# Hybrid decoder on one core: another order of score tiles, key tiles, bias rows and memory work in the mixer, and jobs of projection on both sides of each head's transposes

## The chip, the cores and the metric

The kernel runs on one core of a Trainium2 chip. The time is the device time of one launch in microseconds; lower is better. Engines are named as in the profile: PE is TensorE (matmuls; PEld its weight loads), DVE is VectorE, ACT is ScalarE, POOL is GpSimd, SP issues the loads from memory (DMA).

## What is computed

Two layers on x of 512 tokens by 1024 channels in float32. The change lies in the second of a layer's four parts, the mixer, and in what the mixer prepares for the third.

```python
# per layer
x = x + 0.5 * swiglu(rmsnorm(x, g_ffn1[l]), w_ffn1_gu[l], w_ffn1_down[l])
h = rmsnorm(x, g_mix[l])
zb, zc, zv, zq, zk, zval, zf = jnp.split(h @ w_mix_in[l], SPLITS, axis=-1)
y_conv = zb * causal_depthwise_conv(zc * zv, w_conv[l])          # 512 channels, 3 taps
log_f = jax.nn.log_sigmoid((zf + b_f[l]).astype(jnp.float32))    # 8 heads of 64
# forgetting attention: softmax(q k^T / sqrt(64) + c_t - c_s, causal) v, c = cumsum(log_f)
y_att = forgetting_attention(q, k, v, log_f)
y = jnp.concatenate([rmsnorm(y_conv, g_conv_out[l]), rmsnorm(y_att, g_att_out[l])], axis=-1)
x = x + y @ w_mix_out[l]
x = x + memory_cross_attention(rmsnorm(x, g_xattn[l]), rmsnorm(mem, g_mem[l]), w_xq[l], w_xkv[l], w_xo[l])
x = x + 0.5 * swiglu(rmsnorm(x, g_ffn2[l]), w_ffn2_gu[l], w_ffn2_down[l])
# after the last layer: rmsnorm(x, g_final)
```

## The kernel before

Activations lie transposed, channels on the 128 partitions and 512 tokens along a row. Every product of an activation with a weight is made of float32r matmuls of split operands: `mm3` (L204) does high by high, high by low and low by high, three matmuls of 128x512. `split` (L208 on ACT, L209 on DVE) makes the two halves of an activation; `Weights.prefetch` (L157 on ACT, L158 on DVE) those of a weight unit of 128x1024, two jobs ahead of its use, into three unit buffers. SP loads the raw weights in the order of a list that the kernel writes down ahead of each part (`W.block`).

The kernel is written through a recorder which decides, from the order of the code and from costs of its own, how the instructions of an engine follow one another; each engine then goes through its own list in order. A matmul of a projection can thereby stand between two score matmuls that come earlier in the code.

The mixer first projects v and the forget gate (96 matmuls and `pf`, L778). What is left are jobs of 24 matmuls, in the list `MIX`: q and k of a pair of heads (`head_rows`), or one of the three projections of a conv group (`Conv.step`, L671 to L685). The order is q0 k0 zc0 zv0 zb0 zc1 q1 k1 zv1 zb1 q2 k2 zc2 zv2 q3 k3 zb2 zc3 zv3 zb3. The first five run ahead of head 0 (`MIX_FIRST`); then a loop over h = 0 to 9 does `scores(h)`, some jobs (`MIX_STEP[h]`), `weigh(h - 2)` and `turn(h - 1)`.

- `head_rows`: DVE scales the product (L804). For k, ACT casts the high half of each head's 64 rows (L821), DVE subtracts the low half (L822), ACT copies the high half to the other 64 partitions (L825) and writes the bias rows c times a coefficient next to the low half (L826). So the contraction of a score is over 128 rows, and its two matmuls (e = 0 and 1, L838) need L821 and L825, then L822 and L826.
- `forget_bias` (L701 to L726): from the gate to c by an exp and a log (two ACT table loads, L708 and L709), a scan (L713) and the bias rows of q (L722). It is called in the job k0.
- `scores(h)`: four row tiles t of 128 queries against 128 (t + 1) keys, mask and row maximum on DVE (L840), exp on ACT (L844), reciprocal on DVE (L847), normalising on POOL (L849). By `by_size` the tiles of 128 and 384 keys share one PSUM tile and one SBUF tile.
- `turn(h)`: ten transposes on PE (L859), split on ACT and DVE (L865, L866). `weigh(h)`: eight matmuls of the key tiles kt with v (L875), and L882, L883.
- The memory of the third part: `memory_load` after head 4, `memory_norm` (squares on ACT, L945; L949, L952) after head 6, `memory` (16 transposes, L964; L215, L216) at h = 8, keys (`memory_keys`, matmuls of 128x256, L985, L986) behind the loop, in turn with the sums and the spreading of the two output norms (L391, L395, L407, L411), values behind the output projection.

Of the kernel before, what the change touches and what calls it, by code (L numbers as in the profile page):

```python
# [12 lines left out]
P = 128  # L13
# [5 lines left out]
KD = D // P  # L19
CW = 512  # L20
NT = S // P
NH = 8
# [149 lines left out]
def trunk(ctx, tc, a, consts, out):  # L172
# [14 lines left out]
    def PS():  # L187
        return pspool.tile([P, 512], F32, name="ps", tag="ps")
# [75 lines left out]
    W = Weights(nc, big_pool, unit_pool)  # L264
    for l in range(DEPTH):
        for which in (1, 2):
            gu, dn = a[f"w_ffn{which}_gu"][l], a[f"w_ffn{which}_down"][l]
            if which == 2:
                w_in, w_out = a["w_mix_in"][l], a["w_mix_out"][l]
                W.limit = 4  # L270
                for k in range(4):
                    W.block(w_in, 2 * k, 2, (2560, 512))
                for kind, i in MIX:
                    W.block(w_in, 0, KD, (MIX_COL[kind] + P * i, P))
                for c in range(KD):
                    W.block(a["w_xkv"][l], 0, KD, (P * c, P))
                for c in range(KD):
                    W.block(w_out, 0, KD, (P * c, P))
                for c in range(2):
                    for k in range(4):  # L280
                        W.block(a["w_xkv"][l], 2 * k, 2, (D + 512 * c, 512))
                W.limit = BIG_BUFS - 4
                for n in ("w_xq", "w_xo"):
                    for c in range(KD):
                        W.block(a[n][l], 0, KD, (P * c, P))
                W.slow = 10
            W.limit = BIG_BUFS - 2
            product = {}
            for op, c, i in ffn_plan():
                c0 = sum(CHUNKS[:c])  # L290
                if op == "plain":
                    W.block(gu, 2 * i, 2, (c0, 256), (DFF + c0, 256))
                elif op == "product":
                    if c not in product:
                        product[c] = W.quads(gu, c0, CHUNKS[c])
                    product[c](i)
                elif op == "down" and l == DEPTH - 1 and which == 2 and c == len(CHUNKS) - 1:
                    W.limit = 4
                    W.unit(W.raw(dn, c0 // P + 2 * (i % 2), 2, (512 * (i // 2), 512)), keep=True)
                elif op == "down":  # L300
                    W.block(dn, c0 // P, CHUNKS[c] // P, (256 * i, 256))
# [387 lines left out]
    def scaled(y, norm, base):  # L689

        for i, t in enumerate(y):
            nc.vector.scalar_tensor_tensor(
                out=t, in0=t, scalar=col(base + i), in1=norm.rb, op0=ALU.mult, op1=ALU.mult
            )
            yield split(t)
# [60 lines left out]
    def mixer(l, n, after):  # L756
# [4 lines left out]
        pv = [PS() for _ in range(NT)]  # L761
        wf = None
        for c in range(4):
            w = W.take()
# [18 lines left out]
        v = []  # L783
# [16 lines left out]
        def head_rows(kind, p):  # L800
            ps = PS()
            project(ps, W.take(), n.h)
            t = T()
            nc.vector.scalar_tensor_tensor(  # L804
                out=t, in0=ps, scalar=64 ** -0.5 if kind == "q" else 1.0, in1=n.norm.rb,
                op0=ALU.mult, op1=ALU.mult,
            )
            if kind == "k" and p == 0:
                c.append(forget_bias(l, n, pf, q))
            for b in (0, 64):  # L810
                r, o = slice(b, b + 64), slice(64 - b, 128 - b)
                if kind == "q":
                    nc.scalar.copy(
                        out=q[b][r, :, :], in_=t[r, :].unsqueeze(1).broadcast_to([64, 2, 512])
                    )
                    nc.vector.tensor_tensor(
                        out=q[b][o, 0, :], in0=t[r, :], in1=q[b][r, 0, :].bitcast(F32), op=ALU.subtract
                    )
                else:
                    hi = k[b][r, 0, :]  # L820
                    nc.scalar.copy(out=hi, in_=t[r, :])  # L821
                    nc.vector.tensor_tensor(  # L822
                        out=k[b][r, 1, :], in0=t[r, :], in1=hi.bitcast(F32), op=ALU.subtract
                    )
                    nc.scalar.copy(out=k[b][o, 0, :], in_=t[r, :])  # L825
                    nc.scalar.activation(  # L826
                        out=k[b][o, 1, :], in_=c[0][o, :], func=AF.Copy, scale=coef(6 + p)[o]
                    )

        def scores(h):  # L830
            b = 64 * (h % 2)
            den, inv = SM(NT), SM(NT)
            w, pss = by_size(T(), T(), T()), by_size(PS(), PS(), PS())
            for t in range(NT):
                m = (t + 1) * P
                ts_, o, ps = slice(t * P, m), w[t], pss[t]
                for e in range(2):
                    mm(ps, q[b][:, e, ts_], k[b][:, e, :m], start=not e, stop=e == 1)  # L838
                neg = SM(1)
                nc.vector.tensor_tensor_reduce(  # L840
                    out=o, in0=ps, in1=cst[:, C_MASK + 512 - m : C_MASK + 512],
                    scale=-1.0, scalar=3.0e38, op0=ALU.add, op1=ALU.min, accum_out=neg,
                )
                nc.scalar.activation(  # L844
                    out=o, in_=o, func=AF.Exp, bias=neg, scale=-1.0, accum_out=den[:, t : t + 1]
                )
            nc.vector.reciprocal(out=inv, in_=den)  # L847
            for t in range(NT):
                nc.gpsimd.tensor_tensor(  # L849
                    out=w[t], in0=w[t], in1=inv[:, t : t + 1].broadcast_to([P, (t + 1) * P]), op=ALU.mult  # L850
                )
            wsm[h] = w
# [16 lines left out]
        def weigh(h):  # L869
            p, b = h // 2, 64 * (h % 2)  # L870
            w = wt.pop(h)
            ps = PS()
            for kt in range(NT):
                for e in range(2):
                    mm(  # L875
                        ps[:, kt * P :], v[kt][:, h, :], w[kt][e],
                        start=kt == e == 0, stop=kt == NT - 1 and e == 1,
                    )
            if not b:
                y[p] = T()  # L880
            o = y[p][b : b + 64, :]
            nc.scalar.copy(out=o, in_=ps[64:, :])  # L882
            nc.vector.tensor_add(out=o, in0=ps[:64, :], in1=o)  # L883
            if b:
                norm.add(y[p])
# [3 lines left out]
        def job(n):  # L889
            for _ in range(n):  # L890
                kind, i = jobs.pop(0)
                (head_rows if kind in "qk" else conv.step)(kind, i)

        job(MIX_FIRST)
        for h in range(NH + 2):
            if h < NH:
                scores(h)
            job(MIX_STEP[h])
            if h >= 2:
                weigh(h - 2)  # L900
            if 1 <= h <= NH:
                turn(h - 1)
            if h == 1:
                scale.change(n.norm)
            if h == 4:
                memory_load()
            if h == 6:
                memory_norm()
            if h == 8:
                m = memory(l)  # L910
        n.h = None
        conv.norm.column()
        kT = memory_keys(m, 0, 2)
        conv.norm.spread()
        norm.column()
        kT += memory_keys(m, 2, 2)
        norm.spread()
        yc = list(scaled(conv.y, conv.norm, 88 + 4 * l))
        kT += memory_keys(m, 4, 2)
        ya = list(scaled(y, norm, 96 + 4 * l))  # L920
        kT += memory_keys(m, 6, 2)
        y = yc + ya
        for j in range(KD):
            ps = PS()
            project(ps, W.take(), y)
            nc.vector.tensor_add(out=x[j], in0=ps, in1=x[j])
            after.add(j)
        return kT, memory_values(m)

    mem_in = {}  # L930

# [57 lines left out]
                kT.append((hi[:, e, :], lo[:, e, :]))  # L989
        return kT  # L990

    def memory_values(m):
        v = [[None, None], [None, None]]
        for c in range(2):
            pv = [PS(), PS()]
            for kc in range(4):
                w = W.take()
                for t in range(2):
                    for k2 in range(2):
                        kk = 2 * kc + k2  # L1000
                        mm3(
                            pv[t], [e[:, t * P : (t + 1) * P] for e in m[kk]], [e[:, k2, :] for e in w],
                            kk == 0, kk == KD - 1,
                        )
            for t in range(2):
                v[t][c] = split(pv[t])
        return v

    def cross_attention(l, n, kT, v, after):
        q = [None] * KD  # L1010
# [170 lines left out]
    _HEADS[0] + _CONV[:4] + _HEADS[1] + _CONV[4:6] + _HEADS[2] + _CONV[6:8] + _HEADS[3] + _CONV[8:]  # L1181
)
MIX_FIRST = 5
MIX_STEP = [1, 3, 1, 3, 1, 3, 1, 1, 1, 0]


def ffn_plan():
# [59 lines left out]
```

## Time and profile before

| | us |
|---|---|
| median of 3 runs (lowest, highest) | 2158.92 (2158.47, 2159.44) |
| the profiled execution | 2158.55 |
| its span, first to last instruction | 2156.8 |
| PE busy, share of the span | 2137.7, 99% |
| DVE busy | 1633.3, 76% |
| ACT busy | 1034.5, 48% |
| POOL busy | 94.1, 4% |

The busy share of an engine is an average over the whole kernel. A matmul's record begins when it enters and ends when its last column has left, so that records of matmuls that follow each other overlap. In the rows an idle time before an instruction stands in brackets with the instruction that ended it.

### The profile page before, as it was taken

To read this page: it belongs to the slowest core of one execution; us is meant where nothing else is said; L and a number is where in the kernel's file an instruction comes from. 1 tells how busy PE (TensorE), PEld (TensorE's weight loads), DVE (VectorE), ACT (ScalarE), POOL (GpSimd) and SP (SyncE) were. 2 spreads that over 40 slices of the span, in tenths; PEclk is the share of its full clock that TensorE was granted. 3 is DMA by queue.
4 is the path that set the end of the run, shared out by engine and by line. 5 is a ranking of instruction groups with operands and counts; after the bars stand their busy time and mean duration, and the time that the engine had idled before them with its cause. 6 is when DMAs were issued, how large, how long until landed. Compare 5 with 4: busy or idle time off the path is not lost.

```text
span 2156.8 us, 26234 instructions
## 1 busy us (share of the span) xinstructions
PE 2137.7 (99%) x10110; PEld 1786.1 (83%) x10110; DVE 1633.3 (76%) x2254; ACT 1034.5 (48%) x1550; POOL 94.1 (4%) x107
## 2 busy tenths in 40 slices
PE   9999999999999999999999999999999999999998
PEld 7888888788888888888888888887888888888887
DVE  7987777768755688888788887767786547977785
ACT  7443434566444554444454443346664445434343
POOL 0000000022001000000000000001320010000000
PEclk9999999999999999999999999999999999999999
DMA  5333332123552133333413333502343521333321
GB/s 180 122 108 108 117 99 68 49 79 106 148 138 88 59 108 109 96 98 98 132 58 113 98 108 98 143 24 69 88 127 110 135 79 49 117 108 118 109 77 40
DMA packets 218371, 214.56 MB, mean 99 GB/s; under 512 B 9230, under 2 KB 167174, under 8 KB 218246
## 3 DMA queue, kind: packets, MB, share of 16 engines
q1 hardware_dynamic: 218214, 212.88, 33.3%
q8 instruction: 79, 1.29, 0.2%
q14 instruction: 46, 0.38, 0.1%
q10 hardware_dynamic: 32, 0.01, 0.0%
HBM read 210.77 MB, written 2.10 MB: 99 GB/s over the span
## 4 chain that ended last, share of the span: by engine, by line
PE 92%; DVE 4%; ACT 3%; issue 1%; POOL 0%; DVEq 0%; POOLq 0%; ACTq 0%
PE ps L204 88%; PE ps L579 2%; DVE wlo L158 1%; ACT whi L157 1%; DVE t L866 1%; ACT t L844 1%; PE ps L838 0%; DVE t L685 0%; DVE t L386 0%; PE ps L778 0%; PE ps L1071 0%; DVE t L883 0%; PE ps L875 0%; PE ps L199 0%; PE ps L391 0%
## 5 line engine op out<-in xcount | busy, mean ns | idle before, releaser
L157 ACT CAST whi<-big 128x1024 fp32r<-128x1024 f32 x516 | 536.7, 1040 | 887.5 <-PE ps L204 692.6
L204 PE MATMUL ps<-t,whi 128*128 128x512 f32 x2752 | 851.8, 390 | 0.3
L204 PE MATMUL ps<-whi,t 128*128 128x512 f32 x2624 | 828.7, 390 | 0.2 <-ACT t L208 0.2
L158 DVE TENSOR_TENSOR wlo<-big,whi 128x1024 fp32r<-128x1024 f32 x516 | 623.7, 1211 | 183.7 <-ACT whi L157 181.6
L204 PEld LDWEIGHTS ps<-t,whi 128*128 128x128 f32 x2752 | 514.8, 188 | 106.8 <-DVE t L209 1.6
L204 PEld LDWEIGHTS ps<-whi,t 128*128 128x128 f32 x2624 | 492.6, 188 | 102.8 <-ACT t L208 0.9
L204 PE MATMUL ps<-t,wlo 128*128 128x512 f32 x1376 | 535.7, 389 | 0.0
L204 PE MATMUL ps<-wlo,t 128*128 128x512 f32 x1312 | 510.5, 389 | 0.0
L204 PEld LDWEIGHTS ps<-t,wlo 128*128 128x128 f32 x1376 | 258.3, 188 | 53.5
L204 PEld LDWEIGHTS ps<-wlo,t 128*128 128x128 f32 x1312 | 246.4, 188 | 50.3
L76 DVE TENSOR_TENSOR big<-big 128x1024 f32<-128x1024 f32 x160 | 193.6, 1218 | 1.7
L589 DVE SCALAR_TENSOR_TENSOR x<-ps,x 128x512 f32<-128x512 f32 x184 | 125.0, 686 | 90.2 <-PE ps L204 90.2
L209 DVE TENSOR_TENSOR t<-ps,t 128x512 fp32r<-128x512 f32 x128 | 82.5, 682 | 24.4 <-ACT t L208 24.0
L369 POOL TENSOR_TENSOR s<-s,mhalf 128x4 f32<-128x4 f32 (+1 forms) x19 | 16.4, 863 | 1728.4 <-DVE s L366 1690.6
L208 ACT CAST t<-ps 128x512 fp32r<-128x512 f32 x128 | 70.7, 602 | 26.0 <-PE ps L204 18.6
L849 POOL TENSOR_TENSOR t<-t,s 128x128 f32<-128x128 f32 (+1 forms) x64 | 58.5, 945 | 215.3 <-DVE s L847 181.1
L527 ACT COPY t<-ps 128x512 f32<-128x512 f32 x80 | 45.8, 586 | 34.1 <-PE ps L204 31.3
L844 ACT ACTIVATE t<-t,s 128x128 f32<-128x128 f32 (+1 forms) x64 | 35.4, 555 | 26.4 <-DVE s L840 26.2
L204 PE MATMUL ps<-big,whi 128*128 128x256 f32 x256 | 47.6, 287 | 0.0
L386 DVE TENSOR_TENSOR t<-t 128x512 f32<-128x512 f32 x61 | 44.2, 725 | 1.4 <-ACT t L382 1.4
L579 PE MATMUL ps<-cst,t 128*128 128x128 f32 x352 | 42.3, 272 | 0.0
L579 PEld LDWEIGHTS ps<-cst,t 128*128 128x128 f32 x352 | 39.8, 141 | 3.0
(177 smaller groups left out, 1638.6 us busy)
## 6 DMA issues: line engine op xcount, KB each, us to landing
big<-in_w_ffn_gu SPq DMA_DIRECT2D x160, 512.0 KB, 3.7
big<-in_w_ffn_down SPq DMA_DIRECT2D x80, 512.0 KB, 3.4
big<-in_w_mix_in SPq DMA_DIRECT2D x48, 512.0 KB, 3.9
big<-in_w_xkv SPq DMA_DIRECT2D x32, 512.0 KB, 3.9
big<-in_w_ffn_gu SPq DMA_DIRECT2D x32, 256.0 KB, 3.2
big<-in_w_mix_out SPq DMA_DIRECT2D x16, 512.0 KB, 4.9
big<-in_w_xq SPq DMA_DIRECT2D x16, 512.0 KB, 3.7
big<-in_w_xo SPq DMA_DIRECT2D x16, 512.0 KB, 4.3
```

The lines of the kernel that those rows point to most:

```text
L76: self.nc.vector.tensor_tensor(out=out, in0=a, in1=b, op=op)
L157: self.nc.scalar.copy(out=hi, in_=src)
L158: self.nc.vector.tensor_tensor(out=lo, in0=src, in1=hi.bitcast(F32), op=ALU.subtract)
L204: mm(ps, x, y, start=first and i == 0, stop=last and i == 2)
L208: nc.scalar.copy(out=hi, in_=src)
L209: nc.vector.tensor_tensor(out=lo, in0=src, in1=hi.bitcast(F32), op=ALU.subtract)
L386: nc.vector.tensor_add(out=self.acc, in0=self.acc, in1=sq)
L527: nc.scalar.copy(out=s[i, e], in_=ps)
L579: nc.tensor.transpose(ps[:, t * P : (t + 1) * P], g[t][:, f * P : (f + 1) * P], ident)
L589: nc.vector.scalar_tensor_tensor(out=x[j], in0=ps, scalar=0.5, in1=x[j], op0=ALU.mult, op1=ALU.add)
L844: nc.scalar.activation(out=o, in_=o, func=AF.Exp, bias=neg, scale=-1.0, accum_out=den[:, t : t + 1])
L849: nc.gpsimd.tensor_tensor(out=w[t], in0=w[t], in1=inv[:, t : t + 1].broadcast_to([P, (t + 1) * P]), op=ALU.mult)
```

## The change

The tiles of `scores` are taken in the order 0, 1, 3, 2 and the key tiles of `weigh` in the order 0, 2, 1, 3. `forget_bias` is called in the job q0. `MIX_STEP` now has two numbers for each h: the jobs between `scores(h)` and `weigh(h - 2)`, and those behind `turn(h - 1)`. The memory is loaded, normed and transposed one head earlier, its first two key units come at h = 8, half of its values ahead of the output projection, between whose units the last two attention rows are scaled, and the weight list follows that order.

```diff
-                for c in range(KD):
-                    W.block(w_out, 0, KD, (P * c, P))
                 for c in range(2):
+                    if c:
+                        for i in range(KD):
+                            W.block(w_out, 0, KD, (P * i, P))
                     for k in range(4):
                         W.block(a["w_xkv"][l], 2 * k, 2, (D + 512 * c, 512))
...
-            if kind == "k" and p == 0:
+            if kind == "q" and p == 0:
                 c.append(forget_bias(l, n, pf, q))
...
-            for t in range(NT):
+            for t in (0, 1, 3, 2):
                 m = (t + 1) * P
...
-            for kt in range(NT):
+            for kt in (0, 2, 1, 3):
                 for e in range(2):
...
-            job(MIX_STEP[h])
+            job(MIX_STEP[h][0])
             if h >= 2:
                 weigh(h - 2)
             if 1 <= h <= NH:
                 turn(h - 1)
+            job(MIX_STEP[h][1])
             if h == 1:
                 scale.change(n.norm)
-            if h == 4:
+            if h == 3:
                 memory_load()
-            if h == 6:
+            if h == 5:
                 memory_norm()
-            if h == 8:
+            if h == 7:
                 m = memory(l)
+            if h == NH:
+                kT = memory_keys(m, 0, 2)
         n.h = None
         conv.norm.column()
-        kT = memory_keys(m, 0, 2)
+        kT += memory_keys(m, 2, 2)
         conv.norm.spread()
         norm.column()
-        kT += memory_keys(m, 2, 2)
+        kT += memory_keys(m, 4, 2)
         norm.spread()
         yc = list(scaled(conv.y, conv.norm, 88 + 4 * l))
-        kT += memory_keys(m, 4, 2)
-        ya = list(scaled(y, norm, 96 + 4 * l))
         kT += memory_keys(m, 6, 2)
+        rest, ya = scaled(y, norm, 96 + 4 * l), []
+        ya += [next(rest), next(rest)]
+        mv = [memory_values(m, 0, lambda kc: ya.append(next(rest)) if 0 < kc < 3 else None)]
         y = yc + ya
...
-        return kT, memory_values(m)
+        mv.append(memory_values(m, 1))
+        return kT, list(zip(*mv))
...
-MIX_STEP = [1, 3, 1, 3, 1, 3, 1, 1, 1, 0]
+MIX_STEP = [(1, 0)] + [(1, 1)] * 6 + [(0, 1), (1, 0), (0, 0)]
```

The number of instructions is the same on every engine (PE 10110). The line numbers of the changed mixer are higher by one, so that L839 of it is L838 of before, L822 is L821, L826 is L825, L827 is L826. Three places show how they are ordered.

PE between k of the second pair and the scores of head 2, before. First the end of the k job (ps_3584) and the next one, the projection zv of conv group 1 (ps_3625):

```order
L204 MATMUL ps_3584<-t_3050,whi_3482 128x512
L204 MATMUL ps_3584<-t_3049,wlo_3483 128x512
L204 MATMUL ps_3625<-t_2885,whi_3548 128x512
L204 MATMUL ps_3625<-t_2886,whi_3548 128x512
L204 MATMUL ps_3625<-t_2885,wlo_3549 128x512
```

PE at the end of that zv job, before: ten transposes of head 0, and then the scores of head 2:

```order
L204 MATMUL ps<-t,wlo 128x512
L859 MATMUL ps<-cst,t 128x128 x10
L838 MATMUL ps<-big 128x128 x2
L838 MATMUL ps<-big 128x256 x2
L838 MATMUL ps<-big 128x512 x2
L204 MATMUL ps<-t,whi 128x512 x2
```

The same k job on PE now (ps_3609), with the scores of head 2 (ps_3665 to ps_3667, from the k rows big_3240 and the q rows big_3238) and zv of group 1 (ps_3693):

```order
L204 MATMUL ps_3609<-t_3050,whi_3482 128x512
L204 MATMUL ps_3609<-t_3049,wlo_3483 128x512
L839 MATMUL ps_3665<-big_3240,big_3238 128x128
L839 MATMUL ps_3666<-big_3240,big_3238 128x256
L839 MATMUL ps_3667<-big_3240,big_3238 128x512
L204 MATMUL ps_3693<-t_2885,whi_3548 128x512
L839 MATMUL ps_3665<-big_3240,big_3238 128x128
L839 MATMUL ps_3666<-big_3240,big_3238 128x256
L839 MATMUL ps_3667<-big_3240,big_3238 128x512
L204 MATMUL ps_3693<-t_2886,whi_3548 128x512
L204 MATMUL ps_3693<-t_2885,wlo_3549 128x512
```

The scores of head 2 moved past a job and the transposes, to the end of the k job whose rows they read; heads 4 and 6 stand likewise behind k of pairs 2 and 3.

ACT at k of the last pair, before (t_4202 is the scaled product, big_3240 and big_3241 the rows of the two heads):

```order
L157 CAST whi_4172<-big_3879 128x1024
L157 CAST whi_4213<-big_3920 128x1024
L821 CAST big_3240<-t_4202 64x512
L825 CAST big_3240<-t_4202 64x512
L821 CAST big_3241<-t_4202 64x512
L825 CAST big_3241<-t_4202 64x512
L157 CAST whi_4322<-big_4024 128x1024
```

The same place on ACT now (the product is t_4241; L951 is L945 of before, the square of a memory tile):

```order
L157 CAST whi_4309<-big_3999 128x1024
L951 ACTIVATE t_4252,s_4251<-t_3953 128x512
L822 CAST big_3240<-t_4241 64x512
L826 CAST big_3240<-t_4241 64x512
L822 CAST big_3241<-t_4241 64x512
L826 CAST big_3241<-t_4241 64x512
L951 ACTIVATE t_4254,s_4251<-t_3955 128x512
```

Squares of the memory's norm now stand in front of and behind the four casts.

ACT from the cast of c (L715) to the first exp of head 0, before (t_3324 is c):

```order
L157 CAST whi_3413<-big_3247 128x1024
L715 CAST t_3327<-t_3324 128x512
L683 ACTIVATE t_3408<-t_3406,gcol_83 128x512
L157 CAST whi_3482<-big_3284 128x1024
L826 ACTIVATE big_3240<-t_3324,cst_76 64x512
L826 ACTIVATE big_3241<-t_3324,cst_76 64x512
L382 ACTIVATE t_3446<-t_3443 128x512
L844 ACT_TABLE_LOAD
L844 ACTIVATE t_3450,s_3448<-t_3450,s_3458 128x128
```

The same stretch now (c is t_3287; L814 casts the q rows of head 1, L716 is L715, L684 is L683 and L383 is L382 of before):

```order
L716 CAST t_3290<-t_3287 128x512
L814 CAST big_3239<-t_3273 64x1024
L822 CAST big_3240<-t_3332 64x512
L826 CAST big_3240<-t_3332 64x512
L827 ACTIVATE big_3240<-t_3287,cst_76 64x512
L822 CAST big_3241<-t_3332 64x512
L826 CAST big_3241<-t_3332 64x512
L827 ACTIVATE big_3241<-t_3287,cst_76 64x512
L684 ACTIVATE t_3408<-t_3406,gcol_83 128x512
L157 CAST whi_3413<-big_3247 128x1024
L157 CAST whi_3482<-big_3306 128x1024
L383 ACTIVATE t_3446<-t_3443 128x512
```

The bias rows moved from behind the second weight cast to a place ahead of the convolution's L684.

## Rows read from the trace of the kernel before

**Rows 1.** Page, busy time of each engine.

```profile
PE 2137.7 (99%) x10110; PEld 1786.1 (83%) x10110; DVE 1633.3 (76%) x2254; ACT 1034.5 (48%) x1550; POOL 94.1 (4%) x107
```

**Rows 2.** Windows: stretch, length; busy PE, PEld, DVE, ACT, POOL; PEclk, DMA share, GB/s.

```profile
362.00:635.00 273.00, 268.46 (x1365) 227.22 (x1364) 192.47 (x321) 154.98 (x264) 34.77 (x38) 1.00 0.36 103
635.00:1425.00 790.00, 789.80 (x3639) 657.92 (x3638) 619.76 (x784) 355.98 (x492) 10.28 (x11) 1.00 0.32 97
1425.00:1700.00 275.00, 270.35 (x1372) 228.61 (x1372) 191.93 (x319) 154.99 (x264) 34.84 (x38) 1.00 0.36 102
```

**Rows 3.** Waits of PE: line, waited for, us in total, times, longest us.

```profile
PE ps L838 <- DVE s L840: 4.9, 8, 1.4
PE ps L838 <- ACT big L826: 2.6, 2, 1.3
...
PE ps L407 <- DVE s L401: 0.8, 2, 0.4
PE ps L875 <- DVE t L866: 0.5, 2, 0.3
```

**Rows 4.** Chain that ended last, in order of time: start, us, what.

```profile
1.45 5.20 PE ps L199 x14
...
98.46 59.87 PE ps L204 x264
```

**Rows 5.** Timeline of PE at the first scores: start, us, instruction, [idle before].

```profile
415.90 0.62 PE L838 MATMUL ps<-big 128*128 128x128 f32 x3
...
419.21 0.72 PE L838 MATMUL ps<-big 128*128 128x128 f32 x3 [1.31 <-ACT big L826]
...
425.20 0.39 PE L204 MATMUL ps<-t,whi 128*128 128x512 f32 x1
427.00 0.62 PE L838 MATMUL ps<-big 128*128 128x384 f32 x2 [1.41 <-DVE s L840]
```

**Rows 6.** Timeline of DVE and ACT at the first scores.

```profile
418.44 1.47 ACT L826 ACTIVATE big<-t,cst 64x512 fp32r<-64x512 f32 x2 [1.52 <-DVE t L726]
...
420.73 0.67 DVE L676 TENSOR_TENSOR t<-t 128x512 f32<-128x512 f32 x1
421.33 0.28 DVE L840 CUSTOM_DVE_ANT_0 t<-ps,cst 128x128 f32<-128x128 f32 x1
...
422.08 1.28 ACT L844 ACT_TABLE_LOAD   x1
...
423.90 0.72 ACT L826 ACTIVATE big<-t,cst 64x512 fp32r<-64x512 f32 x1
...
426.58 0.18 DVE L847 RECIPROCAL s<-s 128x4 f32<-128x4 f32 x1 [1.41 <-ACT t L844]
```

**Rows 7.** Timeline of PE, DVE and ACT behind k of pair 1.

```profile
438.15 0.62 PE L204 MATMUL ps<-t,whi 128*128 128x512 f32 x2
...
438.35 0.69 DVE L804 SCALAR_TENSOR_TENSOR t<-ps,t 128x512 f32<-128x512 f32 x1 [1.87 <-PE ps L204]
...
440.35 1.40 DVE L822 TENSOR_TENSOR big<-t,big 64x512 fp32r<-64x512 f32 x2
...
439.09 0.61 ACT L821 CAST big<-t 64x512 fp32r<-64x512 f32 x1
439.72 0.62 ACT L825 CAST big<-t 64x512 fp32r<-64x512 f32 x1
```

**Rows 8.** Timeline of ACT at the memory's norm.

```profile
514.72 0.66 ACT L945 ACTIVATE t<-t 128x512 f32<-128x512 f32 x1
```

**Rows 9.** Timeline of PE at the end of the first mixer's heads.

```profile
533.13 1.01 PE L875 MATMUL ps<-t,big 128*128 128x512 f32 x2
...
536.06 0.34 PE L204 MATMUL ps<-big,whi 128*128 128x256 f32 x1
```

**Rows 10.** Timeline of PE at the end of the kernel.

```profile
2144.65 4.92 PE L204 MATMUL ps<-big,t 128*128 128x512 f32 x21
```

**Rows 11.** Window behind it, columns as in rows 2.

```profile
2152.00:2157.00 5.00, 0.00 (x0) 0.00 (x0) 1.41 (x2) 0.00 (x0) 0.14 (x1) 0.51 0.28 105
```

More of the change, by code (lines that the diff above doesn't have):

```diff
@@ L990, in memory_keys, with memory_values @@
         return kT
[L992 to L1004, printed above, removed]
-            for t in range(2):
-                v[t][c] = split(pv[t])
-        return v
+    def memory_values(m, c, between=lambda kc: None):
+        pv = [PS(), PS()]
+        for kc in range(4):
+            w = W.take()
+            between(kc)
+            for t in range(2):
+                for k2 in range(2):
+                    kk = 2 * kc + k2
+                    mm3(
+                        pv[t], [e[:, t * P : (t + 1) * P] for e in m[kk]], [e[:, k2, :] for e in w],
+                        kk == 0, kk == KD - 1,
+                    )
+        return [split(ps) for ps in pv]
     def cross_attention(l, n, kT, v, after):
```

## The prediction

> **What bounds the kernel now.** The first view to read is the engine table: TensorE (PE) is busy 2137.7 us of a span of 2156.8 [rows 1]. The change adds and removes no matmul, so only PE's idle time can move, and the second view, windows over whole stages, says where that is: in the stretch of the first mixer 273.00 − 268.46 = 4.54 us of PE is not busy, in that of the second 4.65, while the 790 us between them miss 0.20 [rows 2]. The third view names the waits: L838, the score matmuls, waits 8 times for the mask on VectorE (DVE, L840) and twice for the bias rows (ScalarE, L826); with two waits each at L407 and L875 that makes 14 waits and 8.8 us, half in each mixer [rows 3]. A wait costs more than its idle time. A projection matmul has a record of 0.39 us but follows the one ahead every 59.87 / 264 = 0.227 us [rows 4]; a PE that waits has drained the other 0.163. So a mixer's seven waits cost 4.4 + 7 × 0.163 = **5.5 us**. That is all there is to gain at waits; what replaces them decides.
>
> **The first scores.** PE asks for head 0 at 415.90; the second half of its products stands at 419.21 because of L826, 1.31 us [rows 5]. The change puts the forget bias behind the q projection, one job of 24 × 0.227 = 5.4 us earlier, so the rows are written by about 413, and this wait is gone. But the order of the rows of DVE ahead of the first mask hardly shrinks: it now takes the two scaled convolution taps, two weight splits and L675/L676 behind the second half of the q and k rows. Before, the mask starts at 421.33 [rows 6]; adding the same durations in the new order I get 420.75, end 420.98. The tile of 384 keys shares its buffer with that of 128 keys, and may not start until the mask has read the latter. PE, with 1.47 us less behind it, is there after 13 projection matmuls, at about 419.85: a new wait of about **1.2** (nothing if DVE gets ahead by the 0.5 us of L726, 1.9 if it gets ahead by nothing).
>
> Head 1 waits for the mask too, behind the reciprocal of head 0, and that behind L676, the square L382, an exp table load of 1.28 and four exps. Only the bias row of 0.72 that stood between the exps falls out, so the reciprocal comes at 426.58 − 0.76 = 425.82, PE's release at 426.24 instead of 427.00. PE, which came to this wait at 425.20 + 0.227 = 425.43, now comes there at 425.43 − 1.47 + 1.2 = 425.1: **1.1** in place of 1.41 [rows 5, 6] (0.4 to 1.4).
>
> **The jobs in front of the scores.** Here the change costs. Before, between the k projection of a pair and the first scores of that pair's heads (2, 4, 6) stood a conv projection and ten transposes, over 5 us, and PE had no wait there for key rows [rows 3]. After, the first three score matmuls stand directly behind the last k matmul, and PE takes nothing past them. What they need, for k of pair 1: the next matmul could start at 438.15; DVE scales the product at 438.35 for 0.69 us, ScalarE (ACT) casts the high half from 439.09 and copies it to the other half from 439.72, to 440.34 [rows 7]. With 0.05 us to PE (the first of the two L826 ends at 419.16, PE starts at 419.21 [rows 5, 6]) the first score matmul starts at 440.39: **2.24 us lost**. The low half, L822, ends with its first half near 441.05, 2.9 us behind 438.15; three score matmuls and one of projection cover the difference. I take 2.25 each for heads 2 and 4 (2.2 to 2.9: none of the three steps overlaps another, so none can be shorter; the upper end is PE waiting for L822 as well).
>
> For head 6 the order on ACT has an L945 of 0.66 in front of the cast, since the memory's norm now stands one head earlier [rows 8]; it was issued behind the last cast before. That makes 2.25 + 0.65 = **2.9** (2.2 if L945 is through in time, 4 if two stand there). The norm's other work on DVE and ACT also stands in front of the mask of head 6: 0.5 at the tile of 384 (0 to 0.9). Head 7: 0.2, the sort of small mask wait that three heads show before; heads 3 and 5 nothing.
>
> On PE's order the Trainium skill, "TensorE: Matmul & The Clock Gate", section "Step-by-step: what each phase is for", says that only weight loads are pulled ahead and matmuls stay in program order; the trace agrees, since at 419.21 PE had stood 1.31 us with projection matmuls behind [rows 5]. If matmuls could pass, the sum would be that of the first rival.
>
> **The tail.** The last `weigh`, the norm sums and the first memory keys come in one stretch: from 533.13 to 536.06 PE does eight L875 (1.21 as in other heads), four L391 (0.44) and four 128x256 (0.12 each), 2.13 in 2.93 us [rows 9]. With the keys at head 8 and the memory transposed at head 7 the 0.8 us lost there, and the waits at L407 and L875, should go; I leave 0.1. Bounds: nothing to 0.8 won.
>
> **What is hidden.** The new order of value and output weights moves 512 KB loads past one another; no wait of PE for a weight split stands in the mixer [rows 3] and weights are cast two jobs ahead, so I cost it at nothing; the cover is that lead, two jobs of 5.4 us. GpSimd's normalising is done before the transposes in both. The order (0, 2, 1, 3) in `weigh` answers to the order in which `turn` makes its tiles: at most 0.3 us, inside the tail's term.
>
> **The sum**, per mixer: 1.2 + 1.1 + 2.25 + 2.25 + 2.9 + 0.5 + 0.2 + 0.1 = 10.5 us after, against 5.5 and the 0.8 of the tail before: 4.2 us more. Two mixers: **+8.4**. The profiled execution took 2158.55 us (1.75 outside its span; the median of the runs, 2158.92, is 0.37 above): 2158.55 + 8.4 = **2167 us**. With every bound at its low end (0 + 0.4 + 2.2 × 3) the mixer has 7.0, or +1.4 in all: 2160. At the high end (1.9 + 1.4 + 2.9 × 2 + 4 + 0.9 + 0.5, tail unchanged) 14.5, or +18: 2176. All high ends at once are unlikely, but the next rival reaches there too.
>
> **Rivals.**
> 1. The joins of k and scores cost nothing, and the change is faster: PE would fill the gap with the next projection's matmuls. Then a mixer has 10.5 − 7.4 = 3.1 us, 3.2 less than before's 6.3: 2152. It decides at 1.1 us a join: below that the change gains. For it speaks only that those matmuls wait for nothing; against it the 1.31 us at 419.21 [rows 5] and the order, where three score matmuls come first.
> 2. The idle time lowers the clock. After the gaps PE would run at half speed a while. The first 14 matmuls of the kernel take 5.20 us where 14 × 0.227 = 3.2 would do: one spell of 1.2 GHz costs about 2.0 us [rows 4]. At the end PE's last matmul ends at 2149.57 and the granted clock from 2152 on is 0.51 [rows 10, 11]; the longest wait of before, 1.41 us, left it at 1.00 [rows 2, 3]. What the 2.1 to 2.8 us of idle in a join would do, no row shows. All six falling: +12, 2179; head 6's alone: +4, 2171. The same page of the Trainium skill, section "Why this matters for your kernels", has the rule that idle gaps between bursts of matmuls drop the clock; no wait in the mixers of this trace is long enough to show it.
> 3. About no change: the first heads' waits vanish altogether (2.3 less), head 6 has no L945 in front and no mask wait (1.2 less): a mixer of 7.0, 2160 to 2162.
>
> **Chances.** The forecast as it stands (2163 to 2172) 0.62; the clock (2171 to 2179) 0.22; no change 0.09; faster 0.07. The low end 2160 takes in most of the third, the high end 2176 the forecast's bounds and half of the clock's case; about 2 in 10 are left out. A measurement of this kernel can tell 0.2%, 4.3 us, from no change; 2154.6 to 2163.2 is "same". Slower 0.84, same 0.09, faster 0.07.
>
> **What would show it.** In the waits of PE: scores on the key rows of ACT (the copy, L825 of before) six times, some 2.1 us in heads 2 and 4 and 2.7 in head 6; the two waits of 1.3 on bias rows gone; mask waits of about 1 us in heads 0 and 1; none at L407 and L875. The mixers' windows should show PE idle about 9 us instead of 4.5, the clock 1.00 in both. I am wrong if PE starts projection matmuls in the joins, if ACT's casts come later than 2.2 us behind the last k matmul because of other rows in front, or if a window of the mixer shows a granted clock below 1.

## The result and the profile after

The changed kernel takes 2173.8 us in the median (2172.94 to 2176.45, 6 runs) against 2159.01 of before (2158.31 to 2159.45, 6 runs): ratio 1.0071, 95% interval 1.006 to 1.0081, +14.8 us. The forecast was slower, 2167, range 2160 to 2176. The profiled execution took 2173.83, its span is 2172.0, 15.2 more than before.

First the engine table and the waits of PE of the changed kernel, as [rows 1, 3] had them before:

```profile
PE 2142.5 (99%) x10110; PEld 1790.7 (82%) x10110; DVE 1629.8 (75%) x2254; ACT 1035.3 (48%) x1550; POOL 90.1 (4%) x107
```

```profile
PE ps L839 <- ACT big L826: 14.8, 6, 2.7
PE ps L839 <- DVE s L841: 4.6, 5, 1.1
```

In the changed kernel's numbering L826 is the copy of the key rows, L825 of before. PE is busy 4.8 us longer, although it has the same 10110 matmuls: some of them have become slower. And the waits have changed places. The two on bias rows, those at L407 and those at L875 of [rows 3] are gone; six on the key rows have come. With the 0.163 us that each wait adds, 11 waits cost 19.4 + 1.8 = 21.2 us, against 11.1 before; with the 0.8 of each tail gone that is 8.5 more. The places, in the timeline of PE of the first mixer:

```profile
420.93 0.62 PE L839 MATMUL ps<-big 128*128 128x384 f32 x2 [1.08 <-DVE s L841]
426.26 0.62 PE L839 MATMUL ps<-big 128*128 128x384 f32 x2 [1.04 <-DVE s L841]
440.77 0.73 PE L839 MATMUL ps<-big 128*128 128x128 f32 x3 [2.11 <-ACT big L826]
474.72 0.73 PE L839 MATMUL ps<-big 128*128 128x128 f32 x3 [2.69 <-ACT big L826]
508.50 1.19 PE L839 MATMUL ps<-big 128*128 128x128 f32 x6 [2.73 <-ACT big L826]
512.99 0.62 PE L839 MATMUL ps<-big 128*128 128x384 f32 x2 [0.36 <-DVE s L841]
```

These are the joins of the k jobs with heads 2, 4 and 6, and the mask waits of heads 0, 1 and 6. The second mixer has 2.11, 2.42 and 2.73 us at its joins. What is left of the 15.2 us is seen in windows (columns as in [rows 2]): first the three joins of the first mixer, each with the 5 us behind it, then the stretches behind the joins of the second.

```profile
438.00:441.00 3.00, 0.89 (x5) 0.43 (x5) 2.10 (x3) 2.44 (x4) 0.00 (x0) 1.00 0.02 6
441.00:446.00 5.00, 5.00 (x18) 4.07 (x18) 2.92 (x10) 4.06 (x11) 0.00 (x0) 0.66 0.39 108
472.00:475.00 3.00, 0.31 (x3) 0.28 (x3) 3.00 (x5) 2.47 (x4) 0.00 (x0) 1.00 0.39 146
475.00:480.00 5.00, 5.00 (x19) 4.12 (x19) 2.74 (x11) 4.04 (x11) 0.00 (x0) 0.66 0.40 108
505.00:509.00 4.00, 1.27 (x8) 0.81 (x7) 3.44 (x6) 3.47 (x7) 0.00 (x0) 1.00 0.00 1
509.00:514.00 5.00, 4.64 (x22) 3.61 (x22) 2.92 (x11) 3.15 (x10) 1.09 (x2) 1.00 0.38 106
...
1512.00:1517.00 5.00, 5.00 (x24) 4.01 (x25) 3.07 (x11) 4.18 (x11) 0.00 (x0) 1.00 0.41 110
...
1544.00:1549.00 5.00, 4.91 (x17) 4.21 (x18) 3.16 (x10) 3.35 (x9) 0.00 (x0) 0.66 0.39 105
...
1578.00:1583.00 5.00, 5.00 (x18) 4.02 (x19) 2.54 (x10) 3.51 (x10) 1.12 (x2) 0.66 0.36 105
```

In four of the six stretches the granted clock is 0.66 in the mean, although PE is busy in all of it: it falls to 1.2 GHz, the lower of its two levels, after PE has started again, and comes back. 5 x (1 - 0.66) = 1.7 us of clock each, 6.8 in all. 8.5 + 6.8 = 15.3 would meet the 15.2, but in part by luck: the run with work in the joins, below, shows that a fall costs less than its share of clock. The rule of the Trainium skill ("TensorE: Matmul & The Clock Gate", section "Why this matters for your kernels") that idle gaps drop the clock, a rival in the prediction, is borne out by four of six joins, though these idle times, 2.11 to 2.73 us, are shorter than the gaps that the page warns of; here the trace decides.

### The profile page after: what moved, and what is told of

Same layout as the page of the kernel before. It is cut to its first block, busy times and chain, and to the rows that moved or that the text cites. A ratio compares the mean times of both kernels' runs of the same rounds, so it can differ in the third digit from the quotient of the medians.

```text
span 2172.0 us, 26225 instructions
## 1 busy us (share of the span) xinstructions
PE 2142.5 (99%) x10110; PEld 1790.7 (82%) x10110; DVE 1629.8 (75%) x2254; ACT 1035.3 (48%) x1550; POOL 90.1 (4%) x107
## 4 chain that ended last, share of the span: by engine, by line
PE 94%; ACT 2%; DVE 2%; issue 1%; POOL 0%; DVEq 0%; POOLq 0%; ACTq 0%
PE ps L204 89%; PE ps L580 2%; PE ps L876 1%; PE ps L860 1%; PE ps L839 1%; DVE wlo L158 1%; ACT whi L157 1%; PE ps L779 0%; PE ps L1075 0%; PE ps L199 0%; ACT big L826 0%; ACT big L822 0%; PE ps L392 0%; ACT t L845 0%; PE ps L408 0%
## 5 line engine op out<-in xcount | busy, mean ns | idle before, releaser
L204 PE MATMUL ps<-t,whi 128*128 128x512 f32 x2752 | 857.7, 392 | 0.3
L204 PE MATMUL ps<-whi,t 128*128 128x512 f32 x2624 | 828.9, 390 | 0.2 <-ACT t L208 0.2
L204 PEld LDWEIGHTS ps<-t,whi 128*128 128x128 f32 x2752 | 516.6, 189 | 106.4 <-DVE t L209 1.6
L204 PEld LDWEIGHTS ps<-whi,t 128*128 128x128 f32 x2624 | 492.7, 188 | 102.6 <-ACT t L208 0.9
L204 PE MATMUL ps<-t,wlo 128*128 128x512 f32 x1376 | 537.8, 391 | 0.0
L204 PE MATMUL ps<-wlo,t 128*128 128x512 f32 x1312 | 510.8, 389 | 0.0
L204 PEld LDWEIGHTS ps<-t,wlo 128*128 128x128 f32 x1376 | 259.5, 189 | 53.8
L204 PEld LDWEIGHTS ps<-wlo,t 128*128 128x128 f32 x1312 | 246.5, 188 | 50.3
L839 PE MATMUL ps<-big 128*128 128x256 f32 (+3 forms) x128 | 30.3, 356 | 19.6 <-ACT big L826 14.8
L204 PE MATMUL ps<-big,whi 128*128 128x256 f32 x256 | 47.0, 286 | 0.0
L839 PEld LDWEIGHTS ps<-big 128*128 128x128 f32 x128 | 19.7, 200 | 28.9 <-ACT big L826 17.3
```

The lines of the kernel that those rows point to most:

```text
L204: mm(ps, x, y, start=first and i == 0, stop=last and i == 2)
```

## The experiments

All were compared with the kernel before on the same chip; "put back" below means the first of them.

**The jobs put back.**

```diff
-MIX_STEP = [(1, 0)] + [(1, 1)] * 6 + [(0, 1), (1, 0), (0, 0)]
+MIX_STEP = [(n, 0) for n in (1, 3, 1, 3, 1, 3, 1, 1, 1, 0)]
```

> The changed kernel with all jobs of a step ahead of weigh, in the old numbers (1, 3, 1, 3, 1, 3, 1, 1, 1, 0); everything else of the change stays. Theory (the joins of a k job and the scores of its heads cost 2.28 + 2.85 + 2.89 us of PE in a mixer, and the granted clock of 0.5 behind four of the six another 1.7 us each): 2173.8 - 2 x 8.0 - 6.8 = 2151, give or take 2, with no wait on the k rows and the clock 1.00 in both mixers; so the rest of the change is a gain of about 8 us over before. Rival (the bias rows, tile orders and memory work cost most of it): 2160 or more.

2154.37 us (2153.7 to 2155.07), 19.4 less than the changed kernel; against before 0.9978, interval 0.9969 to 0.9987. The waits in the joins, the low clock and the 0.8 us of each tail are gone; the only waits that are left in the mixers are mask waits:

```profile
PE ps L839 <- DVE s L841: 6.4, 10, 1.1
```

So the joins and what follows from them cost 19.4 us and everything else in the change gains 4.7. I had expected 3 us less time, and the result lies outside what I gave. In the first mixer, at heads 3, 5 and 6 the tile of 384 now waits 0.45, 0.21 and 0.61 us for the mask, where the changed kernel had 0.04 at head 3, nothing at head 5 and 0.36 at head 6; the second mixer has 0.45, 0.21 and 0.27. And the falls of the clock cost less than the 1.7 us each that I had put in.

**The jobs alone**, the same edit the other way in the kernel before.

```diff
-            job(MIX_STEP[h])
+            job(MIX_STEP[h][0])
...
+            job(MIX_STEP[h][1])
...
-MIX_STEP = [1, 3, 1, 3, 1, 3, 1, 1, 1, 0]
+MIX_STEP = [(1, 0)] + [(1, 1)] * 6 + [(0, 1), (1, 0), (0, 0)]
```

> The kernel before with the new placement of jobs alone. Theory: the waits of before stay and the joins are added, 2.3 + 2.85 + 2.3 us a mixer (no square of the memory's norm in front for head 6), +15, and two to three falls of the clock in each mixer at 1.7 us, +7 to +10: 2180, between 2176 and 2185, six waits on the k rows. Rival (the placement is not the cause): 2159 to 2165.

2182.36 us (1.0109, interval 1.0096 to 1.0123). The waits of PE show the six joins beside the old waits; a granted clock of about half stood behind five of the six. The placement alone is the loss, 23.2 us here. That is 3.8 more than it costs in the changed kernel: one fall more, and longer waits elsewhere, at L407 1.8 us in place of 0.8.

```profile
PE ps L838 <- ACT big L825: 14.7, 6, 2.7
PE ps L838 <- DVE s L840: 4.7, 6, 1.4
PE ps L838 <- ACT big L826: 2.6, 2, 1.3
PE ps L407 <- DVE s L401: 1.8, 2, 1.4
```

**Work for PE in the joins.**

```diff
+            for _ in range(FILL.get(h, 0)):
+                mm(spun, q[b][:, 0, :P], q[b][:, 0, :], start=True, stop=True)
             for t in (0, 1, 3, 2):
...
+FILL = {2: 9, 4: 11, 6: 11}
```

> The changed kernel with matmuls of no use (128x512 of the q rows into a spare PSUM tile; 9, 11 and 11) between the k job and the scores of heads 2, 4 and 6: PE works through the joins, but the scores start no earlier. Theory (idle time in the joins lowers the clock): the four falls go and the time is 2173.8 - 6.8 = 2167, give or take 1, with the granted clock 1.00 in both mixers. Rival (the clock falls for another reason, or its fall costs nothing by itself): the low clock stays, or goes without gain: 2173 to 2175.

2171.26 us (2170.98 to 2171.8): 2.5 less, not 6.8. The first half of the theory holds: with PE busy in the joins the granted clock is 1.00 all through, here in the windows around the first two joins and the last.

```profile
438.00:446.00 8.00, 7.83 (x36) 5.91 (x35) 5.34 (x13) 6.19 (x13) 0.00 (x0) 1.00 0.33 91
472.00:480.00 8.00, 7.70 (x35) 5.82 (x34) 4.78 (x13) 5.87 (x14) 0.83 (x2) 1.00 0.28 83
...
1574.00:1583.00 9.00, 8.39 (x39) 6.46 (x38) 6.32 (x19) 6.42 (x18) 1.11 (x2) 1.00 0.23 67
```

The price does not. Inside the two mixers the fill gains 3.7 us (traces, from the forget gate's matmuls to the first transposes of the cross-attention: 275.2 and 274.5 us before it, 273.1 and 273.0 with it). Outside them 0.9 of it is lost again in the traces, for a reason that no run shows: three waits at L204 have 0.32 in place of 0.10 us, and one at L1156 (L1154 of the changed kernel) 0.89 in place of 0.45. One piece of the difference shows: a PE at full clock is sooner at the tile of 384 and waits there for the mask.

```profile
475.50 0.62 PE L841 MATMUL ps<-big 128*128 128x384 f32 x2 [0.30 <-DVE s L843]
```

With 62 fillers at 0.227 and ten waits with their 0.163 this kernel has 21.8 us in place of 21.2; four waits of 0.08 to 0.09 us at head 2, too short for the view of waits, cost 1.0 more. So without the falls PE gains 3.7 + 0.6 + 1.0 = 5.3 us, about 1.3 for each, not 1.7. The slow matmuls say the same: in the four stretches of the changed kernel some 25 matmuls of 512 columns followed each other after 0.427 in place of 0.227 us, 5 us in all. With 8.5 + 5.3 some 1.5 of the 15.2 us stay open.

**Another list of jobs**: the conv job that preceded each pair's q and k behind them. As q of the next pair is then written ahead of the odd head's scores, heads 1, 3 and 5 are computed from other q rows.

```diff
-    _HEADS[0] + _CONV[:4] + _HEADS[1] + _CONV[4:6] + _HEADS[2] + _CONV[6:8] + _HEADS[3] + _CONV[8:]
+    _HEADS[0] + _CONV[:3] + _HEADS[1] + _CONV[3:5] + _HEADS[2] + _CONV[5:7] + _HEADS[3] + _CONV[7:]
```

> The changed kernel with the conv job that stood ahead of each pair's q and k moved behind them, so that jobs still stand on both sides of each head's transposes but k is followed by a weighted sum, transposes and a conv job ahead of its first scores. Theory: joins and clock falls are gone as in the run before, 2151; the tile of 384 keys stands right behind that of 512 in four heads, which may cost up to 0.3 us each, so 2151 to 2154. Rival (a job on both sides of the transposes is itself the cost): 2160 or more.

2189.69 us, a miss that says nothing for or against a job on both sides: the scores now follow the q job directly and wait for its low half.

```profile
PE ps L839 <- DVE big L817: 28.5, 6, 6.9
```

q and k of a pair must both lie between the scores of an odd head and the next even one. The same question in an order that keeps this follows.

**A job behind the transposes, but not k.**

```diff
+MIX_STEP = [(1, 0)] + [(2, 1), (0, 1)] * 3 + [(0, 1), (1, 0), (0, 0)]
```

> The changed kernel with two jobs (q and k) between scores and weigh and one behind the transposes at odd heads, one behind them at even heads: (2, 1) and (0, 1). So there are jobs behind the transposes still, but k is followed by a weighted sum, transposes and a conv job. Theory (only k directly ahead of the scores costs): no wait on k rows, clock 1.00, as with all jobs put back, 2154.4, or up to 2 more for the tiles of 384 that now stand among weigh and transposes. Rival (a job behind the transposes costs by itself): 2160 or more.

2158.69 us (0.9997, 0.9988 to 1.0006). No wait on k rows; a job behind the transposes does not cost 15 us. But it is 4.3 us more than with the jobs put back, and more than I had expected: POOL's normalising is late for the transposes of head 6, which have only one job between them and their scores, 1.55 us in each mixer, and behind one of these two waits the clock falls.

```profile
PE ps L839 <- DVE s L841: 5.5, 6, 1.1
PE ps L860 <- POOL t L850: 3.1, 2, 1.5
```

**The memory's norm as before.**

```diff
-            if h == 5:
+            if h == 6:
                 memory_norm()
```

> The changed kernel with the memory's norm at head 6 again, as before. Theory (a square of 0.62 us stands in front of the cast of k rows for head 6, and its DVE work in front of a mask): the join of head 6 falls from 2.89 to about 2.3 and the mask wait of 0.52 in the first mixer goes, 1.6 us in all, and up to two falls of the clock may go with it: 2173.8 - 1.6 = 2172.2, between 2170 and 2173. Rival (head 6 waits for the splits of its transposes, not for the square): 2173.8 and a wait of 2.7 still.

2172.32 us (2172.2 to 2173.36), 1.5 less in the median; the ranges touch. The join of head 6 falls from 2.73 to 2.18 us in both mixers; the square L951 was in front of it. But the gain is not this. The tile of 384 keys of head 7 now waits 0.70 and 0.72 us for the mask, so that all waits on key rows and masks come to 13.8 + 5.6 = 19.4 us, as in the changed kernel; what is gone is one fall of the clock (three joins in place of four).

```profile
508.35 0.73 PE L839 MATMUL ps<-big 128*128 128x128 f32 x3 [2.18 <-ACT big L826]
```

**The parts of the gain.** Four runs apart from the jobs: the bias rows alone and the tail alone (both on the kernel before), and the kernel with the jobs put back without the new order of row tiles and without that of key tiles.

```diff
-            if kind == "k" and p == 0:
+            if kind == "q" and p == 0:
```

> The kernel before with the forget bias in the job q0 alone. Theory (the wait of 1.31 us on bias rows becomes one of 1.07 on the mask at the tile of 384, and the one of 1.42 for head 1 becomes 1.04; 0.6 us a mixer): 2159.1 - 1.2 = 2157.9, between 2157 and 2158.7. Rival (the wait on the bias rows was all that held head 0 back, and goes without a successor): 2156.2 or less.

2157.79 us (ratio 0.9994, 0.9985 to 1.0002): 1.4 less, as expected, though the interval still takes in no change.

> The kernel before with the memory's work and the weight list of the change alone (load, norm and transposes one head earlier, two key units at head 8, half of the values ahead of the output projection); jobs, bias rows and tile orders as before. Theory (0.8 us of the tail and the waits at L407 and L875, 0.57 and 0.42, go in each mixer): 2159.1 - 3.6 = 2155.5, between 2154.5 and 2156.5, with none of these waits left. Rival (the tail is hidden, the gain of the run with the jobs put back lies in the bias rows): 2158 to 2159.5.

2158.52 us (0.9996, 0.9988 to 1.0005): 0.65 less, not 3.6, and not to be told from no change. The waits at L407 and L875 are gone, but a new one stands behind the memory's transposes, until DVE has read the weighted sum (L884):

```profile
524.83 1.91 PE L970 MATMUL ps<-cst,t 128*128 128x128 f32 x16
527.71 0.50 PE L204 MATMUL ps<-t,whi 128*128 128x512 f32 x1 [0.97 <-DVE t L884]
```

The order of row tiles decides it:

```diff
-            for t in (0, 1, 3, 2):
+            for t in range(NT):
                 m = (t + 1) * P
```

> As the run with the jobs put back (2154.4), but the row tiles of the scores in the old order 0, 1, 2, 3. Theory (the late tile of 384 holds up the mask and the exp of the tile of 512 behind it; at head 7 this makes a wait of 1.1 us at the next projection, which the tail alone showed): 2154.4 + 2.4 = 2157, between 2156.3 and 2158, with a wait on L884 of about 1 us in each mixer. Rival (the order of row tiles does nothing, as PE's order is the same): 2154 to 2155.

2156.39 us, 2.0 more than with the jobs put back, and the same wait again:

```profile
526.70 0.50 PE L204 MATMUL ps<-t,whi 128*128 128x512 f32 x1 [0.97 <-DVE t L884]
```

PE's order is the same in both, but on DVE and ACT mask and exp of the 512 keys stand behind those of the late 384 in the old order, and the weight cast, the weight split and L884 behind them. At head 7 the cast starts 2.5 us behind the first matmul of the late tile in the old order and 1.9 in the new, L884 6.4 and 5.1. With (0, 1, 3, 2) only the late tile is late.

```diff
-            for kt in (0, 2, 1, 3):
+            for kt in range(NT):
```

> As the run with the jobs put back (2154.4), but the key tiles of weigh in the old order 0, 1, 2, 3. Theory: the order of the key tiles is worth nothing where weigh stands behind a job, 2154 to 2155. Rival (it makes the difference of 2.7 us between the parts and the whole): 2156 or more.

2153.91 us (2153.49 to 2154.86): the order of the key tiles is worth nothing that these runs can tell. The parts add up to 1.4 + 0.65 + 2.0 = 4.1 of the 4.7 us; the two smaller are no firmer than their intervals.

**Two attempts to go further.** First one more conv job between heads 0 and 1, one fewer between 5 and 6:

```diff
-    _HEADS[0] + _CONV[:4] + _HEADS[1] + _CONV[4:6] + _HEADS[2] + _CONV[6:8] + _HEADS[3] + _CONV[8:]
+    _HEADS[0] + _CONV[:5] + _HEADS[1] + _CONV[5:7] + _HEADS[2] + _CONV[7:9] + _HEADS[3] + _CONV[9:]
...
+MIX_STEP = [(n, 0) for n in (2, 3, 1, 3, 1, 2, 1, 1, 1, 0)]
```

> The changed kernel with the jobs put back ahead of weigh, but two conv jobs instead of one between the scores of heads 0 and 1, and only q and k between those of heads 5 and 6, where weigh and the transposes (2.6 us) are left as cover of the k rows. Theory: the wait of head 1 (1.2 us a mixer) is gone since its softmax has another 5.4 us, and head 6 waits at most 0.3: 2154.4 - 2.4 = 2152, up to 2152.6. Rival (head 1's wait only moves on to the next mask, or head 6 pays): 2154 or more.

2154.47 us, no gain. The wait of head 1 is gone, but the mask wait of head 5 is 0.90 us, and heads 6 and 7 have three of 0.15 to 0.23: the rival. It does show that weigh and transposes alone cover the k rows, but for 0.15 us.

Then a PSUM tile for each score tile:

```diff
-            w, pss = by_size(T(), T(), T()), by_size(PS(), PS(), PS())
+            w, pss = by_size(T(), T(), T()), [PS()[:, : (t + 1) * P] for t in range(NT)]
```

> As the run with the jobs put back (2154.4), but the tile of 384 keys has a PSUM tile of its own, four instead of three for a head. Theory (what is left of waits in the mixer, 4.3 us each with their 0.163, is this tile waiting for the mask of the tile of 128): 2154.4 - 8.7 = 2145.7, between 2145 and 2147.5. Rival (with four of eight PSUM tiles in a head's scores the next job or the transposes wait for one instead): 2150 or more.

2155.26 us (2152.7 to 2156.7): every mask wait is gone, and six others have come, of projections that want a PSUM tile which the weighted sum still holds until L884 has read it. This trace is of an execution of 2152.76 us; three of the eleven lie at 2152.7 to 2152.94, the others at 2154.98 to 2156.7. What those lose is not shown; their mean granted clock, 0.998 in five of the eight against 0.999, leaves a fall behind one of the waits possible.

```profile
PE ps L204 <- DVE t L884: 6.9, 6, 1.8
```

Of the eight PSUM tiles the scores take the one that the next job needs.

## Why the prediction was right, and where it was short

- **The way and the range were right, the forecast's own band was not**: 2173.8 lies above 2163 to 2172, which had 0.62, and in that of the clock, which had 0.22; the range held it because its upper end took in half of the clock's case. Of the signs of being wrong two were seen: a granted clock below 1 in both mixers, and at head 4 casts held up by another row.
- **PE's idle time alone moves the time**: this step failed. The waits came to +8.5 us with the tails, forecast +8.4, but PE was also busy 4.8 us longer with the same matmuls, and of that the forecast's sum held nothing. That the +8.4 fits so closely is in part luck: head 4 cost 0.6 and 0.33 more than its term, while the mask wait of head 6 came in the first mixer alone (0.36 + 0.163 against 0.5) and that of head 7 was 0.07 instead of 0.2.
- **Heads 0 and 1**: 1.08 + 0.163 = 1.24 and 1.20 against 1.2 and 1.1. The wait on the bias rows went and one on the mask took its place, as the order of DVE's rows said.
- **Joins of heads 2 and 6**: 2.27 in place of 2.25, and 2.89 in place of 2.9, of which the run with the norm put back shows 0.55 to be the square.
- **Join of head 4**: 2.85 and 2.58 in place of 2.25. I followed only ACT's list. On DVE the low half of a split of head 2's transposes stands in front of the scaling of k, and the casts of ACT start behind both:

```profile
471.16 1.62 DVE L867 TENSOR_TENSOR t<-ps,t 128x512 fp32r<-128x512 f32 x3 [1.31 <-ACT t L866]
472.69 0.68 DVE L805 SCALAR_TENSOR_TENSOR t<-ps,t 128x512 f32<-128x512 f32 x1
...
473.41 0.62 ACT L822 CAST big<-t 64x512 fp32r<-64x512 f32 x1 [0.48 <-DVE t L805]
474.05 0.62 ACT L826 CAST big<-t 64x512 fp32r<-64x512 f32 x1
```

- **The tail**: the waits and the 0.8 us went, as forecast, but by itself this is worth 0.65, since a wait on L884 comes in its place; only with the new order of row tiles, for which the sum has no term, does the gain stay.
- **Order in PE's list**: PE waited in all six joins, although projection matmuls that waited for nothing followed the first three score matmuls in its list. The first rival fell.
- **The clock**: I gave the second rival 0.22 with six falls at 2.0 us. Four of six came, and they are, with some 5.3 us, the larger part of the 6.8 us between 2167 and 2173.8. This is the step that was short: the likeliest case had no term for what idle time does to the matmuls behind it, although the longest wait known to leave the clock at 1.00 was 1.41 us, shorter than any join.

Open stays why one join lowers the clock and the next does not, and some 1.5 us of the loss.

## What to carry to other kernels

When an order is changed, follow the chain from the last matmul of a producer to the first of its reader over every engine's list (here scale, cast, copy, with what stands in front of each), and ask how many other matmuls lie between: here 2.2 us of work on two other engines, which a weighted sum and ten transposes cover. A wait of PE longer than any that the trace shows to be harmless is to be priced with the matmuls behind it, which may run at the lower clock (here some 1.3 us for a fall). And edits that each seem worth little can hold each other's gain: the tail's work paid only where the late score tile no longer stood in front of others.

The best version is the changed kernel with the jobs put back: 2154.4 us (2153.9 with the old key tiles, which is no clear difference), 4.7 less than before and 19.4 less than the change as it was made.

## What the runs showed of the hardware

The clock does not follow the length of a single wait. After the same 2.11 us of idle time at the join of head 2 it was 0.66 in the mean in the first mixer (441 to 446) and 1.00 in the second (1512 to 1517); after 2.73 us at head 6 it was 1.00 in the first (509 to 514) and 0.66 in the second (1578 to 1583). In this kernel PE had been at work again for 0.3 to 1.3 us each time when it fell. Longer waits fared worse: in the run with another list of jobs it fell behind all four waits of 3.69 us, and within both of 6.9 us. With a job behind the transposes it even fell behind a wait of 1.55 us, once, in the second mixer, and not behind the same wait in the first (windows behind the two, columns as in [rows 2]):

```profile
1580.00:1584.00 4.00, 4.00 (x17) 3.80 (x18) 2.00 (x8) 1.81 (x6) 0.00 (x0) 0.57 0.00 2
...
518.00:522.00 4.00, 4.00 (x25) 3.55 (x24) 2.68 (x10) 2.83 (x10) 0.00 (x0) 1.00 0.02 4
```

So a wait does not have to be as long as those of the joins. The runs of the changed kernel, 2172.94 to 2176.45 us, spread wider than those of before, and follow their mean granted clock: 0.997 at 2172.94 and 2173.09, 0.996 at 2173.8, 0.995 at 2176.45.
